# The last store of an x-minus-mean-squared kernel cut into a 62 KiB and a 2 KiB part per partition

## The chip, the cores and the metric

One core of one Trainium2 chip. The time is the device time of one execution in microseconds (us).

## The reference

```python
batch, dim = 1024, 4096          # x is float32
mean = np.mean(x, axis=-1, keepdims=True)
return ((x - mean) ** 2).astype(np.float32)
```

16.8 MB are read and 16.8 MB written.

## The kernel before

Each of 128 partitions handles eight rows, in two tiles of four rows, so a tile has 64 KiB per partition. All loads are issued at the start. VectorE (DVE) forms each row's negative mean; ScalarE (ACT) squares with it as bias; the last 512 columns of each tile go to VectorE. One store per tile, issued by SyncE (SP), ends each tile.

```python
    for i in range(ntiles):                      # ntiles = 2, Q = 4, D = 4096, HEAD = 512
        x_tile = io.tile([P, Q * D], F32)
        if i == 0:
            nc.sync.dma_start(out=x_tile[:, :HEAD], in_=x_t[i][:, :HEAD])
            nc.sync.dma_start(out=x_tile[:, HEAD:], in_=x_t[i][:, HEAD:])
        else:
            end = Q * D - HEAD
            nc.scalar.dma_start(out=x_tile[:, end:], in_=x_t[i][:, end:])
            nc.sync.dma_start(out=x_tile[:, :end], in_=x_t[i][:, :end])
        tiles.append(x_tile)
    # ... (pools, row loop: tensor_tensor_reduce on DVE, Square on ACT)
            cut = D if q < Q - 1 else LAST       # LAST = D - 512
            # ...
            if cut < D:
                rest = row[:, cut:]
                nc.vector.tensor_scalar_add(out=rest, in0=rest, scalar1=neg_mean)
                nc.vector.tensor_mul(out=rest, in0=rest, in1=rest)
        nc.sync.dma_start(out=out_t[i], in_=tiles[i])
```

## Time and profile before

| | before |
|---|---|
| time, median of the first three runs | 82.99 us |
| span of the profiled run | 81.37 us |
| DVE and ACT busy | 20.8 and 29.4 us |
| large DMA queue, share of 16 engines' span | 95.0% |
| last store issued; landed | 58.36; 80.58 us |

Three parts of the profile matter: SP's waits, which tell what the kernel's end waits for; the packets and the rate in GB/s; and the single packet records in the trace. The last are printed by no view; I read them from the trace, one record per run that a DMA engine moved (start, duration, bytes), with 16 records of 4 bytes at the end of each transfer (96 for the six transfers of the kernel before). I call these the engines' completion writes. The records don't name their engine: "first" and "last" below are the first and the last of the 16 in time. "Landing" is the last of a transfer's 16 semaphore counts in the trace (for the last store 0.348 us behind the last completion write). Here are the two waits of SP ahead of the stores, from the waits of the kernel before (columns: who waited for what; us in total, times, longest us):

```profile
SPq L88 <- DVE x_tile L87: 41.8, 2, 29.4
SPq L88 <- ACT x_tile L77: 11.7, 2, 5.8
```

The stores wait last for ACT (5.8 us after DVE is done, for each tile). The wait named DVE is the longer one only because it is counted first: for the first store it runs from 4.4 to 33.9 us, and the 5.8 us for ACT follow it. The compute engines then idle through the second store (0.00 us busy from 60.90 us on).

### The profile page before, as it was taken

What the parts mean: (1) busy time and instruction counts of PE and PEld (TensorE: products, weight loads), DVE (VectorE), ACT (ScalarE), POOL (GpSimd) and SP (SyncE); (2) the same over time, 40 slices, a digit from 0 to 9 for tenths busy, and PEclk for the clock granted to TensorE, in tenths of its full rate; (3) what the DMA queues carried; (4) which work ended last, traced back from release to release, by engine and by line L of the source; (5) the groups of instructions that cost most, each with busy time, mean ns of one, the idle gap of its engine ahead of it and who ended that gap; (6) DMA issues with size and microseconds to landing.
All of it is one profiled execution on the core that took longest, in us unless ns stands there. A gap on an engine that the chain in (4) does not pass through costs nothing.

```text
span 81.4 us, 87 instructions
## 1 busy us (share of the span) xinstructions
DVE 20.8 (26%) x20; ACT 29.4 (36%) x9; POOL 0.2 (0%) x4
## 2 busy tenths in 40 slices
DVE  0000000000059999600039999700000000000000
ACT  0000000000054999999502999999600000000000
POOL 0000000000000000000000000000000000000000
DMA  1974999999759999995799993899996599999390
GB/s 22 704 343 187 499 499 499 499 499 437 343 218 499 499 499 499 499 406 250 343 516 515 515 515 161 354 515 515 515 516 290 258 483 515 515 515 419 161 451 0
DMA packets 864, 33.55 MB, mean 412 GB/s; under 512 B 96, under 2 KB 96, under 8 KB 352
## 3 DMA queue, kind: packets, MB, share of 16 engines
q1 hardware_dynamic: 720, 33.29, 95.0%
q10 hardware_dynamic: 144, 0.26, 1.1%
HBM read 16.78 MB, written 16.78 MB: 412 GB/s over the span
## 4 chain that ended last, share of the span: by engine, by line
DMA 49%; ACT 13%; ACTq 4%; DVE 3%; SPq 1%; issue 0%
DMA x_tile<-in_x_dram 49%; ACT x_tile L77 13%; ACTq L119 4%; DVE pairs L66 3%; SPq L53 1%; SPq L52 0%; DVE neg_mean L66 0%
## 5 line engine op out<-in xcount | busy, mean ns | idle before, releaser
L77 ACT ACTIVATE x_tile<-x_tile,neg_mean 128x4096 f32<-128x4096 f32 (+1 forms) x8 | 28.2, 3590 | 5.7 <-DVE neg_mean L66 5.7
L66 DVE CUSTOM_DVE_ANT_0 pairs<-x_tile 128x2048 f32<-128x2048 f32 x8 | 18.3, 2292 | 31.6 <-DMA x_tile<-in_x_dram 31.4
L77 ACT ACT_TABLE_LOAD x1 | 1.3, 1283 | 23.2 <-DMA x_tile<-in_x_dram 23.2
L87 DVE TENSOR_TENSOR x_tile<-x_tile 128x512 f32<-128x512 f32 x2 | 1.4, 692 | 0.1
L86 DVE TENSOR_SCALAR x_tile<-x_tile,neg_mean 128x512 f32<-128x512 f32 x2 | 1.0, 488 | 0.1
L66 DVE DVE_READ_ACCUMULATOR2_ANT neg_mean<- 128x1 f32 x8 | 0.7, 82 | 0.0
L105 POOL MEMSET const-bfloat16-1.0<- 128x1 bf16 x1 | 0.1, 102 | 0.0
L105 POOL MEMSET const-uint8-127<- 128x1 uint8 x1 | 0.1, 102 | 0.0
L105 POOL MEMSET const-float32-0.0<- 128x1 f32 x1 | 0.1, 99 | 0.2 <-issue 0.2
L105 POOL MEMSET const-float32-1.0<- 128x1 f32 x1 | 0.1, 99 | 0.0
## 6 DMA issues: line engine op xcount, KB each, us to landing
x_tile<-in_x_dram SPq DMA_DIRECT2D x2, 7936.0 KB, 31.1
x_tile<-in_x_dram ACTq DMA_DIRECT2D x1, 256.0 KB, 3.8
x_tile<-in_x_dram SPq DMA_DIRECT2D x1, 256.0 KB, 3.6
out_dram<-x_tile SPq DMA_DIRECT2D x2, 21.9
```

The lines of the kernel that those rows point to most:

```text
L53: nc.sync.dma_start(out=x_tile[:, HEAD:], in_=x_t[i][:, HEAD:])
L66: inorder(nc.vector.tensor_tensor_reduce(out=pairs, in0=row[:, :HALF], in1=row[:, HALF:], scale=-inv_d, scalar=0.0, op0=ADD, op1=ADD, accu ...
L77: nc.scalar.activation(out=row[:, :cut], in_=row[:, :cut], func=ACT.Square, bias=neg_mean, scale=1.0,)
L86: nc.vector.tensor_scalar_add(out=rest, in0=rest, scalar1=neg_mean)
L87: nc.vector.tensor_mul(out=rest, in0=rest, in1=rest)
L105: nc = _bacc.Bacc("TRN2", target_bir_lowering=False, num_devices=1)
L119: with _tile.TileContext(nc) as tc:
```

## The change

Its intent is to end the kernel on a short transfer: the last store becomes one DMA with all but the last 512 columns, and behind it one with those 512.

```diff
-        nc.sync.dma_start(out=out_t[i], in_=tiles[i])
+        cuts = [0, Q * D - HEAD, Q * D] if i == ntiles - 1 else [0, Q * D]
+        for lo, hi in zip(cuts, cuts[1:]):
+            nc.sync.dma_start(out=out_t[i][:, lo:hi], in_=tiles[i][:, lo:hi])
```

## The prediction

> **What bounds the kernel now**
>
> I read the page's summary first, then the chain that ended last, then the waits of the DMA queue's issuer (SP), then the timeline around the last store, then busy time by stage, and at last the packet records of the trace one by one. The page:
>
> ```profile
> DVE 20.8 (26%) x20; ACT 29.4 (36%) x9; POOL 0.2 (0%) x4
> DMA  1974999999759999995799993899996599999390
> ...
> DMA packets 864, 33.55 MB, mean 412 GB/s; under 512 B 96, under 2 KB 96, under 8 KB 352
> ...
> q1 hardware_dynamic: 720, 33.29, 95.0%
> ...
> out_dram<-x_tile SPq DMA_DIRECT2D x2, 21.9
> ```
>
> No compute engine is busy for more than 36% of the span; the one large queue, q1, is busy for 95% of what 16 engines could give. (A record is put wholly into the slice where it starts, so the single digits of the DMA row jump; the 95% does not.) The 864 packets are the place where this change lands: 512 of them are the 62 KiB and 64 KiB runs of the four big transfers, 256 the 2 KiB runs of the two small loads ("under 8 KB 352" less the 96 completion writes of 4 bytes).
>
> The chain that ended last stops at a compute instruction and must be read with care:
>
> ```profile
> 1.64 40.26 DMA x_tile<-in_x_dram
> 41.90 0.02 issue
> 41.92 2.29 DVE pairs L66
> ...
> 51.56 3.60 ACTq L119
> 55.16 3.17 ACT x_tile L77
> ```
>
> It has nothing after 58.3 us, although the span is 81.4 us. What lies there shows in SP's waits and in the stages:
>
> ```profile
> SPq L119 <- DMA out_dram<-x_tile: 21.7, 2, 19.3
> ...
> 58.36 0.34 SPq L88 DMA_DIRECT2D out_dram<-x_tile  x1
> ...
> 23.20:41.90 18.70, 10.38 (x10) 15.36 (x5) 0.00 (x0) 1.00 1.01 436
> 41.90:60.90 19.00, 10.38 (x10) 14.08 (x4) 0.00 (x0) 1.00 1.02 442
> 60.90:79.50 18.60, 0.00 (x0) 0.00 (x0) 0.00 (x0) 1.00 0.91 395
> 80.24:81.37 1.13, 0.00 (x0) 0.00 (x0) 0.00 (x0) 1.00 0.00 0
> ```
>
> The wait at the program's end for the last store is one of 19.3 us, and no engine computes from 58.3 us on. The last store's issue starts at 58.36 us, but the completion writes of the store before it start between 60.25 and 60.88 us: a fresh store needs some 1.20 us from issue to first packet (the first store: issue 39.73, first packet 40.93), so the last one's descriptors were ready at about 59.56 us, 0.7 us before the first engine was free. From there the end is set by 16 DMA engines, each with eight 64 KiB runs, and the path behind them.
>
> The packet records give that path to the nanosecond. Per engine the last store's completion write follows that of the store before by 19,319 ns (first to first: 60,247 to 79,566) to 19,351 ns (last to last: 60,879 to 80,230). The last completion write starts at 80.230 us, its semaphore lands at 80.578 (0.348 us later), SP sees it at 80.594, and the closing barrier takes the rest to 81.37: 0.79 us after the landing.
>
> [...]
>
> [...]8 x 65,536 B in 19,319 ns is 27.14 B/ns per engine, 434 GB/s over 16.[...]
>
> [...]The median record of a 2 KiB load run is 84 ns[...].
>
> [...]rebuilt per engine, consecutive big records overlap by 3 to 4 ns, and where a completion write lies between two transfers the gap is +1 to +4 ns, so a completion write costs about 6 ns and drains nothing.
>
> [...]In this trace the receipt is 0.35 to 0.46 us (completion write to landing, last store) and the start 1.2 us; both are there once per chain of transfers, not once per transfer, if the next one is already queued.
>
> **The change part by part**
>
> Removed: one store of 64 KiB per partition (eight 65,536 B descriptors per engine, one completion write). Added: one store of 62 KiB per partition, then one of 2 KiB (eight and eight descriptors, two completion writes), on the same SP queue. The instruction order on DVE, ACT and POOL is unchanged; SP has one issue more. The 62 KiB store waits for ACT alone and the 2 KiB store for DVE; but ACT ends last (about 58.34 us; DVE's last product ends at 52.48), so the first part can't start earlier.
>
> 1. The 62 KiB part. I size it from the loads, which have just these runs: completion write of the first big load to that of the second, 22,182 to 40,898 = 18,716 ns for eight runs and one completion write. Loads and stores go at the same rate here: 18,716 x 65,536 / 63,488 = 19,320, which is the store's 19,319. So a 62 KiB store should take 18,716 ns per engine.
> 2. The 2 KiB part. Eight runs per engine at 80 ns (the median record of 84 less the overlap of about 4): 640 ns. This is the one number taken from loads that no store shows.
> 3. One completion write more: 6 ns.
> 4. Sum per engine: 18,716 + 640 + 6 = 19,362 ns, against 19,319 to 19,351 before: +11 to +43 ns. I take +0.04 us: the bytes are the same, and eight descriptors more at 4 to 5 ns make it.
> 5. The issue of the second part, 0.34 us of SP, comes at about 58.75 us and its data are due after 79 us: hidden with 20 us to spare.
> 6. The closing path: one semaphore more to be waited for. SP's closing steps after the last landing are 0.05 to 0.07 us apart (80.594, 80.662, 80.717), so this is 0 if the new wait shares a step, else some 0.05 us. I take +0.02.
> 7. The receipt: 0.35 us as before.
>
> Sum: +0.06 us on 82.99, that is 83.05 us.
>
> **The rivals**
>
> Small stores are dear. If a 2 KiB run to HBM took two or three times the load's 80 ns, eight of them add 0.64 to 1.3 us: 83.7 to 84.3. For it: the trace has no 2 KiB store, and the runs lie at a pitch of 128 KiB. Against: the 2 KiB loads have the same pitch and 84 ns is their median; the long ones (up to 589 ns) are at the start-up of the kernel, where both queues were empty.
>
> Each small run waits for its own receipt. Eight receipts of 0.35 us in place of 0.64 us would be +2.2 us: 85.2, the only way I see to "slower". Against: the overlap of 3 to 4 ns between records, and the +2 ns at a completion write between two stores.
>
> The receipt gets shorter, or the engines even out. The 16 engines' last completion writes are spread over 0.66 us (79.57 to 80.23); if small runs at the end let the late ones catch up, up to about 0.3 us could go: 82.7. Against: each engine has its own fixed runs, eight big and eight small, so a late engine stays late; and with 2 KiB loads the receipt is about the same (completion writes from 3.38 us, landings from 3.74 us).
>
> The first part starts earlier because its wait no longer names DVE. DVE has been done 5.9 us before ACT, and the engines would be occupied anyway: worth nothing.
>
> **Range and chances**
>
> The time before repeats within 0.03 us, so the range comes from the size of the 2 KiB stores and of the closing path. Low: nothing added and 0.07 us less receipt, 82.92. High: 2 KiB stores at about 115 ns a run, +0.3 us, 83.35. A slowdown over 2% is +1.66 us, or 290 ns per 2 KiB run on every engine: 2%. A gain over 2% has no source in the trace, since bytes and rate stay: 1%. Within 2%: 97%.
>
> **What would show it right or wrong**
>
> In the changed kernel's profile: 1,008 packets (864 + 128 data runs + 16 completion writes), "under 8 KB" 496; the last store's 62 KiB records at about 2,342 ns and the 2 KiB ones at about 84 ns; the span between completion writes of the first store and of the 2 KiB store 19.32 to 19.40 us per engine; the last landing about 0.35 us behind the last completion write; SP's closing wait still one of some 19.3 us in all. The first store and everything before 58.36 us unchanged. Wrong it would be if the 2 KiB records stand at 150 ns or more, if a gap opens between the 62 KiB part and the 2 KiB part (a drain, or descriptors not yet there), or if the closing steps behind the last landing grow by over 0.1 us.

The forecast's sum came to +0.06 us, 83.05 us: +0.04 us for the stream (18,716 + 640 + 6 ns against 19,319 to 19,351) and +0.02 us for the closing path. The "4 to 5 ns" a run of item 4: the trace of the kernel before gives that figure, as an estimate of mine. With eight runs an engine and one completion write in both, the 64 KiB store took 19,319 ns and the 62 KiB load 18,716, so 2,048 B of a run take 603 / 8 = 75.4 ns (27.2 B/ns), and a 2 KiB run of 80 ns is 4.6 ns over its bytes. That each engine has its own eight runs shows in the same records: chained by end and start they make 16 chains, each with eight 64 KiB records ahead of its last completion write; and the engines' completion writes are spread over 0.63 us at the first store and 0.66 us at the last, so the late ones don't catch up.

## The result, and the profile after

Six runs of each: 83.02 us median after (82.95 to 83.32), 82.97 before (82.86 to 82.99). The ratio is 1.0014 with a 95% interval of 0.9998 to 1.003. (A ratio is the mean time of one kernel's fast runs over that of the other's of the same rounds, so it is not quite the ratio of the medians.) This is the same time, at most 0.3% slower.

From the page of the changed kernel, packets and issues (columns of the issue lines: KB of one DMA where known, us from issue to landing):

```profile
DMA packets 1008, 33.55 MB, mean 413 GB/s; under 512 B 112, under 2 KB 112, under 8 KB 496
...
q1 hardware_dynamic: 864, 33.29, 95.0%
...
out_dram<-x_tile SPq DMA_DIRECT2D x1, 7936.0 KB, 21.6
...
out_dram<-x_tile SPq DMA_DIRECT2D x1, 256.0 KB, 21.8
out_dram<-x_tile SPq DMA_DIRECT2D x1, 21.5
```

The counts are the predicted ones (1,008 packets, 496 under 8 KB), with the same bytes and the same share of the span. The 256 KB store takes 21.8 us from issue to landing, and this is no cost: it stands in the queue nearly all of that time, each engine works on it for 0.65 us only, and the receipt takes 0.35 us. From its timeline (start us, us, what), then from SP's waits, then from its stages (stretch, its length, busy us of DVE, ACT and POOL, clock, DMA share, GB/s):

```profile
58.25 1.57 SPq L91 DMA_DIRECT2D out_dram<-x_tile  x2
```

```profile
SPq L122 <- DMA out_dram<-x_tile: 20.5, 3, 18.6
```

```profile
41.90:60.90 19.00, 10.28 (x10) 14.08 (x4) 0.00 (x0) 1.00 1.02 440
60.90:79.50 18.60, 0.00 (x0) 0.00 (x0) 0.00 (x0) 1.00 0.90 391
79.50:80.24 0.74, 0.00 (x0) 0.00 (x0) 0.00 (x0) 1.00 0.38 144
```

The issue line holds the one surprise: two issues of 0.34 us each would be 0.7 us, and the two took 1.57 us. Their own durations in the trace are 0.344 and 1.179 us. SP ends at 59.8 us and has nothing to do until 79.8 us, so it is off the path. SP's wait for stores is now in three pieces: the first store, the 62 KiB part (18.6 us), the 2 KiB part. In the stages, 79.50 to 80.24 us now shows a DMA share of 0.38 where the kernel before has 0.01: a record counts where it starts, and the short ones start there. The line of the kernel before:

```profile
79.50:80.24 0.74, 0.00 (x0) 0.00 (x0) 0.00 (x0) 1.00 0.01 0
```

The packet records from 58 us on, per engine (16 of each completion write; from the trace, not a view of the profile):

```
                                              before          after
first store's completion writes, us       60.247-60.879   60.049-60.719
62 KiB part's completion writes               -           78.771-79.452
last completion writes                    79.566-80.230   79.416-80.098
first store's to the last, ns, first/last 19,319/19,351   19,367/19,379
62 KiB part, ns, first/last                   -           18,722/18,733
median record of a 2 KiB run, ns              -               84
last completion write to last landing, ns      348             348
last landing to the end of the span, ns        790             812
```

Read in this order, it is the prediction's sum: the engines' path grew by 48 (first to first) and 28 ns (last to last), the receipt by 0, the closing by 22 ns. How well such a number repeats is seen in the other traces that hold these stores. On the average of the 16 engines, the last stretch of the table (first store's completion write to the last) is 19,346 ns before and 19,384 after; the second trace of the changed kernel (the run "again" below) has 19,398 ns, and a last store left whole took 19,319 ns in two further traces (no_heads, early_first). So the cut adds 38 to 79 ns, by the traces compared, and the forecast for this stretch, 11 to 43 ns, lies at the lower end of that. The span of this one profiled run is 0.11 us *shorter* than before (81.26 against 81.37), only because its loads began and ended earlier (last landing of a load 41.78 against 41.90 us). A difference of this size can't be read from two spans, but it can, to some 30 ns, from the stretch that the change touches.

### The profile page after: what moved, and what is told of

It reads as the page before. It is cut to its first block, busy times and chain, and to the rows that moved or that the text cites. A ratio compares the mean times of both kernels' runs of the same rounds, so it can differ in the third digit from the quotient of the medians.

```text
span 81.3 us, 88 instructions
## 1 busy us (share of the span) xinstructions
DVE 20.7 (26%) x20; ACT 29.4 (36%) x9; POOL 0.2 (0%) x4
## 2 busy tenths in 40 slices
DMA packets 1008, 33.55 MB, mean 413 GB/s; under 512 B 112, under 2 KB 112, under 8 KB 496
## 3 DMA queue, kind: packets, MB, share of 16 engines
q1 hardware_dynamic: 864, 33.29, 95.0%
## 4 chain that ended last, share of the span: by engine, by line
DMA 49%; ACT 13%; ACTq 4%; DVE 3%; SPq 1%; issue 0%
DMA x_tile<-in_x_dram 49%; ACT x_tile L78 13%; ACTq L122 4%; DVE pairs L67 3%; SPq L54 1%; SPq L53 0%; DVE neg_mean L67 0%
## 6 DMA issues: line engine op xcount, KB each, us to landing
out_dram<-x_tile SPq DMA_DIRECT2D x1, 256.0 KB, 21.8
```

## The experiments

Eleven runs, in three sessions, each session with its own runs of the kernel before. The diffs are cut to the lines that matter; they are against the changed kernel, or, where that is said, against the kernel before. The first theory: the DMA engines' stream sets the end, each run costs its bytes at 27.2 B/ns plus 4 to 5 ns, each completion write 6 ns, and nothing else is added. (The first two are the estimate beside the prediction, from the 62 KiB, 64 KiB and 2 KiB runs of the kernel before; the third is the step from an overlap of 3 to 4 ns between records to a gap of 1 to 4 ns at a completion write, in the same trace. The expectations use the same figures.) The rivals: the 2 KiB part has a fixed cost of its own; short stores are dear; the place at the end matters.

### again: the change, measured once more

No edit.

> The changed kernel once more, for a narrower interval. Theory (only eight runs and one completion write more per engine, 4 to 6 ns each): +0.03 to +0.07 us against before, 83.0 us. Rival (the slower run of 83.32 is typical, a cost outside the DMA stream): +0.15 us or more.

83.29 us against 83.16 (median of 11 runs), ratio 1.0010, interval 0.9992 to 1.0027. Its profiled run fell on its slowest run. Together with the first ratio, +0.08 to +0.12 us are the best values and +0.04 is inside both intervals; +0.15 isn't excluded either. The clock can't resolve the forecast 0.06 us. The packet records of this run show +52 ns of stream on the average engine (19,398 against 19,346 ns) and +22 ns of closing, a little more than in the first trace.

### no_tail: the 62 KiB part alone

Wrong on purpose: the last 512 columns are never written.

```diff
-        cuts = [0, Q * D - HEAD, Q * D] if i == ntiles - 1 else [0, Q * D]
+        cuts = [0, Q * D - HEAD] if i == ntiles - 1 else [0, Q * D]
```

> The 62 KiB store alone; the last 512 columns of each partition stay unwritten, so the result is wrong on purpose. Theory: the 2 KiB part costs 8 x 80 + 6 = 646 ns in the stream and nothing else, so -0.60 us against before and -0.65 us against the change. Rival (the small part has a fixed cost of its own, start or receipt): -0.9 us or more against the change. Rival (the small part is hidden): the same as before.

82.58 us against 83.16, ratio 0.9929 (0.991 to 0.9948): -0.59 us, and the theory said -0.60. So the 2 KiB part, which lands 21.8 us after its issue, is worth its 0.65 us in the stream and no more: neither hidden nor burdened with a start or a receipt of its own. The clock alone only just excludes the rival: against the change the two ratios make it -0.67 us, give or take 0.2. The 645 to 646 ns between the two completion writes of an engine in the change's trace, with the receipt unchanged, are the stronger evidence. From the page of this kernel:

```profile
span 80.6 us, 87 instructions
...
DMA packets 864, 33.29 MB, mean 413 GB/s; under 512 B 96, under 2 KB 96, under 8 KB 352
```

A 256 KB transfer less (33.29 MB against 33.55) at the same 413 GB/s.

### halves: as many runs more, none of them short

```diff
+        cuts = [0, Q * D // 2, Q * D] if i == ntiles - 1 else [0, Q * D]
```

> The last store as two DMAs with runs of 32 KiB: just as many runs and completion writes more as in the change, but none short. Theory (the count of runs is what costs): as the change, +0.03 to +0.07 us against before. Rival (it is the short run that costs): +0.00 to 0.02 us, below the change by 0.04 us or more.

83.21 us against 83.16, ratio 1.0009 (0.9991 to 1.0028), the change's ratio in the same session being 1.0010. The clock agrees with the theory but can't exclude the rival, 0.04 us apart. The records can: first store to the last completion write is 19,362 (first) and 19,363 ns (last), in the change 19,367 and 19,379; on the average engine 19,381, in the change's two traces 19,384 and 19,398. So eight runs and a completion write more cost the same with 32 KiB as with 2 KiB, within the scatter of single traces. From the page of this kernel (no store run is under 8 KB):

```profile
DMA packets 1008, 33.55 MB, mean 412 GB/s; under 512 B 112, under 2 KB 112, under 8 KB 368
```

### tail_512B: the short part in four

```diff
+        cuts = [0] + list(range(Q * D - HEAD, Q * D + 1, HEAD // 4)) if i == ntiles - 1 else [0, Q * D]
```

> The 2 KiB part cut into four DMAs of 512 B per partition: 32 runs and four completion writes per engine in place of 8 and one. Theory: 32 x (512 / 27.2 + 4.5) + 4 x 6 = 770 ns in place of 646, so +0.12 us against the change, +0.17 us against before. Rival (a run has a floor of about 80 ns however short): 32 x 80 = 2,560 ns, +1.9 us against the change.

83.48 us against 83.12, ratio 1.0044 (1.0031 to 1.0057): +0.37 us, where +0.17 was expected. The short part itself is right: from the 62 KiB part's landing to the last one's it is 762 (first) and 771 ns (last), against 770 expected; a 512 B record is 27 ns, not 80, so the rival's floor isn't there. What I left out lies on both sides of it. The closing stretch from last landing to end is 913 ns against 790: two more of SP's waits, in steps of 0.06 us, follow the last landing. This kernel has ten DMAs in place of the change's seven; why these two waits come so late was not shown. And the 62 KiB part, during whose first 3.6 us the issues of the short ones still go on (five issues, 58.33 to 63.79 us), took 18,769 (first) to 18,825 ns (last) in place of 18,722 to 18,733: the first two records of each engine are 2,365 and 2,372 ns on average, where the later ones are some 2,346. From its timeline:

```profile
58.33 5.46 SPq L91 DMA_DIRECT2D out_dram<-x_tile  x5
```

### act_queue: the short part on ACT's queue

```diff
+            queue = nc.scalar if lo else nc.sync
+            queue.dma_start(out=out_t[i][:, lo:hi], in_=tiles[i][:, lo:hi])
```

> The 2 KiB part issued on the ACT queue right after ACT's last activation. Its packets then go between those of the first store or the 62 KiB part, not behind them. Theory (an engine's total is what counts, wherever the packets stand): as the change, within 0.05 us. Rival (place at the end matters, the last receipt behind a short run is another than behind a long one): 0.1 us or more away from the change. Also told: whether the issue of the 2 KiB part takes 0.35 us on an empty queue or 1.18 us again.

83.34 us against 83.12, ratio 1.0017 (1.0005 to 1.0029). It did not come behind ACT's last activation, as I had written: it waits for DVE alone and was issued at 52.39 us, as the timeline shows. Its packets stand between those of the first store, from 57.81 to 61.31 us.

```profile
52.39 0.35 ACTq L92 DMA_DIRECT2D out_dram<-x_tile  x1
...
58.24 0.34 SPq L92 DMA_DIRECT2D out_dram<-x_tile  x1
```

Twenty microseconds away from the end it costs what it costs at the end: +0.14 us by this ratio, +0.08 to +0.12 for the change, and the intervals overlap widely. And each issue is 0.34 to 0.35 us, so in these runs the 1.18 us stand only where a store was issued directly behind another on one queue, as in the change.

### tail_first: the short part ahead of the long one

```diff
+        for lo, hi in list(zip(cuts, cuts[1:]))[::-1]:
```

> The same two DMAs, the 2 KiB one first (it waits for DVE alone and can be issued at 52.5 us), the 62 KiB one behind it. Theory: as the change, within 0.05 us. Rival (the end behind a 62 KiB run is earlier or later than behind a 2 KiB run): 0.1 us or more away. If the long issue of 1.18 us [...]falls on the 62 KiB part here, that part is ready at about 60.5 us, and engines free from 60.1 us would idle up to 0.5 us: +0.1 to +0.4 us.

83.22 us against 83.12, ratio 1.0010 (0.9998 to 1.0022): as the change. The end behind a 62 KiB run is no other than behind a 2 KiB run. The two issues were 52.43 (0.344 us) and 58.29 us (0.332 us), so the feared late start didn't arise: not back to back, none was long.

### all_2K: the whole last store in 2 KiB runs

Against the kernel before; the lines stand under `if i == ntiles - 1:`, and the first store stays as it was.

```diff
+            o = out_t[i].rearrange("p (c t f) -> p t c f", t=2, f=HEAD)
+            s = tiles[i].rearrange("p (c t f) -> p t c f", t=2, f=HEAD)
+            for t in range(2):                     # even runs, then odd runs
+                nc.sync.dma_start(out=o[:, t], in_=s[:, t])
```

> The whole last store in runs of 2 KiB, as two DMAs with the even and the odd runs: 256 runs per engine in place of 8. Theory: 256 x 80 + 12 = 20,490 ns per engine against 19,319 to 19,351, so +1.15 us, 84.1 us. Rival (short runs cost little more than their bytes when queued): +0.3 us. Rival (stores of 2 KiB are dear in number[...]): +2 us or more.

85.79 us against 83.16, ratio 1.0314 (1.0294 to 1.0334): +2.61 us, and not +1.15. This was a miss by the theory's own numbers. From the page of this kernel:

```profile
GB/s 16 718 423 363 242 423 484 484 484 484 484 484 423 302 242 484 484 484 484 499 499 312 250 437 499 499 499 499 25 387 384 370 389 390 383 382 390 389 385 119
DMA packets 4848, 33.55 MB, mean 399 GB/s; under 512 B 112, under 2 KB 112, under 8 KB 4464
```

In the last quarter of the row the rate settles at 382 to 390 GB/s, with one slice of 370. At 80 ns a run, 16 engines would move 16 x 2,048 / 80 = 410 GB/s; 386 GB/s is 84.8 ns a run. The completion writes say the same: 128 runs took 10,814 to 10,971 ns from one to the next, about 84.8 ns each, the median record being 88 ns where the change's tail has 84. So 256 x 4.8 = 1.23 us of the excess; the base of 1.16 us stands; and the first store's last records, during which the second issue was going on (58.8 to 64.3 us), were 2,545 to 2,698 ns in place of 2,418, which adds 0.23 us on the average engine from first packet to completion write (0.13 us on the first). The sum is about 2.6 us. From its timeline, the two issues:

```profile
58.38 5.88 SPq L93 DMA_DIRECT2D out_dram<-x_tile  x2
```

### six_2K: is it the pitch or the number of short runs?

```diff
+        cuts = [0] + list(range(Q * D - 6 * HEAD, Q * D + 1, HEAD)) if i == ntiles - 1 else [0, Q * D]
```

> The last store as one DMA with runs of 52 KiB and six with runs of 2 KiB per partition: 48 short runs and six completion writes more per engine. It asks why a 2 KiB run took 84.8 ns in the kernel with all runs of 2 KiB and 80 ns in the change. Theory A (80 ns is the pace when an engine goes from partition to partition, and the pitch of 4 KiB within a partition made it 84.8): 646 ns from completion write to completion write, as in the change; the six cost 48 x 4.7 + 6 x 6 = 0.26 us, plus up to 0.1 us from the long issues and 0.06 us per wait at the end that comes after the last landing: +0.25 to +0.5 us against before. Theory B (80 ns holds for the first eight only, and the pace falls in a long row of short runs): 680 ns and more per piece from the second or third on, +0.5 to +0.8 us.

83.84 us against 83.07, ratio 1.0089 (1.0076 to 1.0102): +0.74 us, as theory B has it. The 2 KiB records, by when they started (from the trace):

```
started, us    records in 0.3 us   mean ns   median ns
76.1-76.4             26             84.2       84
76.4-76.7             57             84.4       84
77.0-77.3             57             86.9       87
77.9-78.2             57             87.6       88
79.4-79.7             55             88.1       88
80.0-80.3             46             85.3       84
80.3-80.6             17             83.9       84
the change, 79.1-79.4 45             84.0       84
```

Here an engine goes from partition to partition, as in the change, and the runs slow down all the same, so the pitch of 4 KiB isn't the cause (theory A falls). The pace drops while all 16 engines do short runs at once (55 to 57 records in 0.3 us) and comes back when engines drop out. In the change the engines reach their short part spread over 0.68 us and leave it after 0.65 us, and there it stayed at 84 ns. But being all at it is not enough: at 76.4 us the 16 engines already start 57 records in 0.3 us and the mean is still 84.4 ns, and in the second trace of the change 54 start in 0.3 us (79.4 to 79.7 us) with a mean of 84.1. The drop came after 0.6 us of it. So what the records show is a slowing that came after 0.6 us of short runs on all engines; its cause is open, and no run tested it. The size: the stream took 19,690 to 19,768 ns in place of 19,319 to 19,351, +0.4 us. The closing stretch is 1,050 ns in place of 790, +0.26 us (the two make 0.66 of the 0.74 us; the rest is within the scatter of the runs), again with waits behind the last landing (80.924 us): SP steps through five, at 80.94, 80.99, 81.06, 81.12 and 81.18 us. The timeline shows seven issues back to back:

```profile
58.38 7.95 SPq L91 DMA_DIRECT2D out_dram<-x_tile  x7
```

### early_first: an attempt to beat both kernels

The engines have small gaps between the last load and the first store (in the kernel before 6 to 142 ns from the loads' completion writes to the store's first packets, each in order of time; the expectation has 0.04 to 0.24 us, which is too much). I tried to fill them by storing three rows of the first tile early (against the kernel before).

```diff
+            if i == 0 and q == Q - 2:
+                done = (q + 1) * D
+                nc.sync.dma_start(out=out_t[i][:, :done], in_=tiles[i][:, :done])
+        lo = (Q - 1) * D if i == 0 else 0
+        nc.sync.dma_start(out=out_t[i][:, lo:], in_=tiles[i][:, lo:])
```

> Not the change: the last store stays one DMA and the FIRST is split, rows 0 to 2 (48 KiB runs) issued when ACT has squared row 2 (about 36.5 us), row 3 behind them. In the kernel before the first store is issued at 39.73 us, its first packets come at 40.93 us, and the loads' completion writes lie at 40.90 to 41.50 us against first store packets that start, in the same order, 0.04 to 0.24 us later. Theory (the only waits left in the stream are there): -0.05 to -0.25 us against before, in spite of eight runs and one completion write more. Rival: the gap moves to the second store, which is then needed earlier than its descriptors are ready (59.56 us against some 60.0 us): no gain.

84.46 us against 83.12, ratio 1.0177 (1.0153 to 1.0202): both theories missed. Its chain of waits (start us, us, what) against that of the kernel before, where the loads' piece is 40.26 us long:

```profile
1.63 42.11 DMA x_tile<-in_x_dram
43.74 0.02 issue
43.77 2.29 DVE pairs L67
```

The loads end 1.85 us later. In the packet records, the last load run of every engine is 3,424 to 4,048 ns long in place of 2,342, on average 1.43 us more, and all earlier ones are as before. The gap that I wanted to fill went, and a larger one appeared inside the record before it.

### early_act: the same on ACT's queue

As early_first, but for this line:

```diff
+                nc.scalar.dma_start(out=out_t[i][:, :done], in_=tiles[i][:, :done])
```

> The early part of the first store again (rows 0 to 2, 48 KiB runs), issued on the ACT queue and so not behind the last loads in their ring. With it on SP's queue the last load record of each engine grew from 2,342 to 3,424 to 4,048 ns. Theory A (a store ready behind a load in the same ring holds up the load's end): with its own ring the load records stay at 2,342 ns, or share the engine with the store's in equal parts, and the time is at or below before, 82.8 to 83.1 us. Theory B (loads and stores together on an engine are slower in sum, whichever ring): +1 us or more again.

84.76 us against 83.07, ratio 1.0199 (1.0181 to 1.0217). The last load records are again long, 3,500 to 4,058 ns, and the store's first packets start only behind them, at 42.25 us. So it isn't the common ring (queue), for the early store's bytes are on q10 here (6.55 MB with the small load) and the large loads' on q1: theory A falls. Theory B says "together on an engine", and that is not quite it either, as the next run shows. From the chain of waits, then from the timeline:

```profile
1.64 43.38 DMA x_tile<-in_x_dram
...
61.49 0.34 SPq L93 DMA_DIRECT2D out_dram<-x_tile  x1
```

The loads now land 3.13 us later than in the kernel before. The long records are 1.50 us of that on average; the rest is that on each engine one 48 KiB run of the store (1,815 ns) went between the last load run and its completion write, which came at 44.06 to 44.64 us. ACT then ends later and the second store is issued only at 61.49 us. Its first packets start at 62.33 to 62.48 us, 0.84 to 0.99 us behind the issue, and the engines stood idle for 0.3 to 0.7 us.

### no_heads: without the small loads

Against the kernel before:

```diff
-        if i == 0:
-            nc.sync.dma_start(out=x_tile[:, :HEAD], in_=x_t[i][:, :HEAD])
-            nc.sync.dma_start(out=x_tile[:, HEAD:], in_=x_t[i][:, HEAD:])
-        else:
-            ...                                    # the two loads of the second tile
+        nc.sync.dma_start(out=x_tile, in_=x_t[i])
```

> Not the change: the last store stays whole, and instead the small loads at the start go; each tile is loaded by one DMA with runs of 64 KiB. In the kernel before an engine's 16 runs of 2 KiB take from 1.75 us to 3.4 to 4.07 us, where their bytes need 1.2 us at 27.2 B/ns[...]. Theory (what is on the stream of the engines is paid in full, wherever it stands): -0.4 to -1.0 us, 82.2 to 82.8 us. Rival (the start is a latency that the first long run pays just so): within 0.1 us of before.

83.20 us against 83.07, ratio 1.0021 (1.0002 to 1.0041): no gain, as the rival said.

From its page, then from its timeline:

```profile
DMA packets 576, 33.55 MB, mean 412 GB/s; under 512 B 64, under 2 KB 64, under 8 KB 64
```

```profile
39.09 19.68 SPq L82 DMA_DIRECT2D out_dram<-x_tile  x2
```

With 288 packets fewer than before the rate is the same. The first long run of each engine takes 2,604 to 3,359 ns in place of 2,418, so most of the time that the small runs lost at the start is lost in the long ones just so, and the second load's completion writes come at 40.95 to 41.61 us (before: 40.90 to 41.50). One thing more: here the first store was issued at 39.09 us, 1.86 us and more ahead of the loads' completion writes (a start from idle engines took 0.84 to 0.99 us in early_act), and the last load records are at most 2,432 ns. A store that is ready behind a load is thus not enough to stretch it. In the two early kernels the store was issued (36.75 and 36.38 us) before the last load runs began (38.5 us), here (39.09 us) while they were under way or about to be (they start at 38.53 to 39.18 us). Whether that is the condition, no run tested.

No version of mine beat the two kernels.

## Why the prediction was right

1. *The 62 KiB part, 18,716 ns an engine.* Right: 18,722 to 18,733. Loads were the right yardstick for stores of the same run.
2. *The 2 KiB part, 8 x 80 = 640 ns.* Right: records of 84 ns, 645 to 646 ns with its completion write, and taking it away alone gave -0.59 us. The yardstick was good for this dose only: with all engines in short runs for long, 84.8 ns (all_2K).
3. *One completion write more, 6 ns,* and *the sum, +11 to +43 ns.* Measured +28 to +48 ns between the first two traces, +38 to +79 ns on the average engine over all of them. The direction and the order of size are right, the exact term isn't resolved. halves agrees that the number of runs makes it, not their length (19,381 ns on the average engine with 32 KiB runs, 19,384 and 19,398 with 2 KiB ones).
4. *The second issue, 0.34 us of SP, hidden.* Hidden it was; the 0.34 us was wrong, it took 1.18 us. I had taken a store's issue from one that stood alone.
5. *The closing path, +0.02 us.* Measured +0.022, but this is luck: it is not where the prediction put it. SP's new wait cost nothing, since the 62 KiB part had landed before (waits at 79.838 and 80.463 us, and from the last landing to SP's second drain 139 ns in both kernels). The 22 ns come later, on GpSimd: its clearing of the semaphores took 92 ns in place of 74 and the drain ahead of it 70 in place of 66 (from the trace, in both traces of the change). The two misses tail_512B and six_2K show what waits cost that do come late: with two and five of them behind the last landing the closing grew by 0.12 and 0.26 us.
6. *The receipt, as before.* 348 ns in both. A reading beside it was wrong without harm: the 1.20 us from a store's issue to its first packet. That store stood behind loads, so it is no start time; in the change's trace the same store's first packet came 1.13 us after its issue, 6 ns behind a load's completion write, and the one store that found idle engines (early_act) took 0.84 to 0.99 us. A store was thus ready to start even earlier than the prediction says.
7. *The rivals.* "Small stores are dear" fell with the 84 ns and with no_tail; "each run waits for its own receipt" fell with the same 84 ns (512 B runs even 27); "the receipt gets shorter, or the engines even out" fell with 348 ns and with a spread of the last completion writes of 0.68 us against 0.66 (0.79 in again). That the first part starts earlier fell with its issue, 58.25 us against 58.36, where ACT, too, ended 0.11 us earlier.

The total, 83.02 us against 83.05 predicted, is closer than the runs can tell: the range rested on a scatter of 0.03 us among three runs, and in the next session eleven runs of the kernel before spread over 0.45 us. The trace shows the parts, to some 30 ns; the clock only that they add up to less than 0.3 us.

## What to carry to other kernels

When the DMA engines' stream ends the kernel and the pieces are queued in time, as here, cutting a transfer costs its extra runs (here 38 to 79 ns of stream for eight runs and a completion write on each engine) and gains nothing (83.02 us against 82.97): what ended last was the sum of each engine's work, wherever the short piece stood (ratios 1.0017 in act_queue, 1.0010 in tail_first). Size a split from the records of one engine and from the steps after the last landing, not from issue-to-landing times (21.8 us for a piece worth 0.65 us) and not from two spans. And measure at the dose that you mean to use: 2 KiB runs were nearly free by the eight and cost 3% of the kernel by the 256.

## What the runs showed beside the forecast

- 256 KiB as a DMA of its own, queued behind another, cost 0.65 us (the change), its bytes alone being 0.60 (8 x 75.4 ns, from the estimate beside the prediction). Four of just 64 KiB, queued, cost 0.19 us each (tail_512B), of which 0.15 are bytes by the same estimate.
- The change's 2 KiB runs took 4.6 ns over their bytes (80 ns less 75.4, the same estimate). With all 16 engines storing 2 KiB runs for over 20 us (all_2K) it was 9.4 ns (84.8 less 75.4).
- Alone, a store's issue was 0.34 us; directly behind another store 1.18 us for 8 runs per engine, 1.17 to 1.28 us in rows of four to six (tail_512B, six_2K), and 5.44 us for 128 behind 128 (all_2K). The loads issued back to back at the start took 0.38 to 0.43 us each.
- A store issued two load runs ahead of the loads' end stretched the last load run of each engine from 2.34 to 3.4 to 4.06 us, from either queue (early_first, early_act), and one issued as the last runs began did not (no_heads, at most 2.43 us).
- SP's waits at the end can come behind the last landing: in six_2K five of them followed it, in steps of some 0.06 us.
